# Placing the tiles of a hybrid decoder trunk at multiples of 128 bytes, with weight tiles stepped by 16 bytes from chunk to chunk

## The chip, the cores and the metric

The kernel runs on one core of one Trainium2 chip. The metric is the device time of one execution in microseconds. Three timed runs of the kernel before gave 645.31, 649.29 and 649.80 us, so the median is 649.29 us.

## The reference

The reference is a two-layer decoder trunk on one sequence of 256 tokens and 1024 features, all in float32. Layer 0 has an RMSNorm, one input projection shared by a softmax attention (8 heads of 64; with 256 tokens and blocks of 256 only the own causal block counts) and a gated linear attention (8 heads), one output projection and a residual add. Layer 1 has an RMSNorm, a projection to a gate branch and a recurrent branch (width-4 causal convolution, two block-diagonal gates, a linear recurrence over the tokens), an output projection and a residual add. After each of the two comes a gated feed-forward block, and it holds most of the arithmetic:

```
h = causal_dwconv(x @ w_up, conv_w, conv_b)      # 1024 -> 6144 columns, width 3
u, g = split(h, 2);  return (u * gelu(g)) @ w_down   # 3072 -> 1024
```

A final RMSNorm ends it. The weights are read once from device memory, some 107 MB in all.

## The kernel before

Activations lie transposed, features on the 128 partitions and the 256 tokens along the free dimension. All large weight matrices are cut on the host into 204 chunks of 128 partitions by 1024 float32 columns (4096 bytes of each partition) in the order in which they are used. A matrix product with close to float32 accuracy is made of three passes in the type fp32r: each weight chunk `w` is split into a high part `wh` (ScalarE, line 134) and a low part `wl = w - wh` (VectorE, line 135), the activations likewise into X[:, k, 0, :] and X[:, k, 1, :], and `passes` (lines 141 to 148) issues for each 128x128 block the products high-high, high-low and low-high. Each is one weight load of 128 columns (PEld in the profile) and one matmul with 256 moving columns (PE), so a chunk is 24 weight loads and 24 matmuls, and all 204 chunks are 4896 of the 5218 matmul records. In nearly all products the weight chunk is the stationary operand and the activations are the moving one; in `tok_gemm` (`pst` in the profile, 192 matmuls) it is the other way round.

`load_w` keeps a look-ahead of one chunk in program order; `issue_w` allocates the tiles: `w` from a ring of 4, `wh` and `wl` from rings of 6 each (a separate ring of 10 for the ten chunks from 104 on). Every transfer of a chunk goes through the queue of SP (line 127). The tile framework packs all tiles into the partition by their lifetimes. Within the rings it reuses addresses as they come free, and a tile that takes the place of another waits for the readers of that one. The order of instructions on each engine is set by the framework's own planner from its estimate of times, with a few orders forced by hand (`order`).

What the change touches is where tiles start. The framework places each tile at a multiple of 32 bytes. The tile `big` (line 80) is 2678 columns, 10,712 bytes, rounded to 10,720, which is 96 more than a multiple of 128. It starts at byte 98,432 of the partition (769 x 128), so what is packed directly behind it starts at byte 109,152, which is 852 x 128 + 96, and since chunks are 4096 bytes, all the `w`, `wh` and `wl` tiles in that region lie 96 bytes past a multiple of 128. A few chunks are placed ahead of `big`, in room that other tiles have left, and start at a multiple of 128. In the program as it is laid out:

| start past a multiple of 128 | chunks of 204 |
|---|---|
| `wh` 96, `wl` 96 | 174 |
| `wh` 96, `wl` 0 | 14 |
| `wh` 0, `wl` 96 | 6 |
| `wh` 0, `wl` 0 | 10 |

The ten are chunks 106, 124, 141, 147, 153, 159, 165, 171, 177 and 183; seven of them are in the up-projection of the second feed-forward block, one in every six chunks. The activations X, M and the `y2` of the feed-forward blocks all start at a multiple of 128 bytes, and every slice of them that a matmul reads does too.

Other tiles that the change touches are small: the 2-column tiles of the norms and the softmax (lines 189, 516, 521), the 8-column tiles of the recurrence constants (line 366) and one of 16 columns (line 576).

Of the kernel before, what the change touches and what calls it, by code (L numbers as in the profile page):

```python
# [8 lines left out]
F32 = mybir.dt.float32  # L9
F32R = mybir.dt.float32r  # L10
# [12 lines left out]
P = 128  # L23
S = 256
D = 1024
KT = 8
# [3 lines left out]
CW = 1024  # L30
# [18 lines left out]
NV = _o  # L49
# [13 lines left out]
def trunk(ctx: ExitStack, tc: tile.TileContext, xT, w, wgk, wgk2, vec, cst, mskf, out):  # L63
    nc = tc.nc

    cp = ctx.enter_context(tc.tile_pool(name="cp", bufs=1))
    wp = ctx.enter_context(tc.tile_pool(name="wp", bufs=4))
    xp = ctx.enter_context(tc.tile_pool(name="xp", bufs=1))
    tp = ctx.enter_context(tc.tile_pool(name="tp", bufs=2))
    pp = ctx.enter_context(tc.tile_pool(name="pp", bufs=1, space=bass.MemoryType.PSUM))  # L70

    def bank(name, tag="g"):
        return pp.tile([P, 512], F32, tag=tag, bufs=BANKS[tag], name=name)

    def order(first, then):
        tc.add_manual_dep(then.ins, first.ins.name,
                          mybir.DependencyInfo(mybir.DependencyClass.NoSync, mybir.DependencyReason.DATA),
                          reason="issue order")

    big = cp.tile([P, KT * S + P + NV + 8], F32, name="big")  # L80
    h = big[:, 0:KT * S].rearrange("p (k t) -> p k t", k=KT)
    idt = big[:, KT * S:KT * S + P]
    vt = big[:, KT * S + P:KT * S + P + NV]
# [22 lines left out]
    def act(name, *args, **kw):  # L106
        use(name)
        ins = nc.scalar.activation(*args, **kw)
        order(tbl["load"], ins)
        tbl["ops"].append(ins)  # L110
        return ins
# [6 lines left out]
    def load_w():  # L118
        while len(state["q"]) <= LOOK and state["i"] < NCH:
            state["q"].append(issue_w())  # L120
        return state["q"].pop(0)

    def issue_w():
        i = state["i"]
        state["i"] += 1
        wt = wp.tile([P, CW], F32, tag="w", name=f"w{i}")
        dma = nc.sync.dma_start(wt, w[i])
        if i == 0:
            first.append(dma)
        pre = "p" if L1_C0 <= i < L1_C0 + NPRE else ""  # L130
        nb = NPRE if pre else 6
        wh = wp.tile([P, CW], F32R, tag="wh" + pre, bufs=nb, name=f"wh{i}")
        wl = wp.tile([P, CW], F32R, tag="wl" + pre, bufs=nb, name=f"wl{i}")
        hi = nc.scalar.activation(wh, wt, AF.Copy)  # L134
        lo = nc.vector.tensor_sub(wl, wt, wh.bitcast(F32))  # L135
        for kind, o in (("h", hi), ("l", lo)):
            for before in state["hooks"].pop((kind, i), []):
                order(before, o)
        return wh, wl
# [24 lines left out]
    class Norm:  # L164
# [18 lines left out]
        def rstd(self, copy=True, hook=0):  # L183
            ps = bank("nps", "t")
            for t in range(2):
                for i, s_ in enumerate(self.acc):
                    nc.tensor.matmul(ps[:, t:t + 1], s_[:, t * P:(t + 1) * P], ones, start=i == 0,
                                     stop=i == len(self.acc) - 1)
            rt = tp.tile([P, 2], F32, tag="rtk", name="rtk")
            root = act(SQRT, rt, ps[:, 0:2], AF.Sqrt, bias=epst, scale=1.0 / D)  # L190
            inv = nc.vector.reciprocal(rt, rt)
            for t in range(2):
                nc.tensor.transpose(ps[:, S + t * P:S + (t + 1) * P], rt[:, t:t + 1].to_broadcast([P, P]), idt)
            self.tok = rt
            if not copy:
                return ps[:, S:2 * S]
            rs = tp.tile([P, S], F32, tag="rs", name="rs")
            cp_ = nc.scalar.activation(rs, ps[:, S:2 * S], AF.Copy)
            if hook:
                for key, o in zip((("h", hook), ("l", hook), ("h", hook + 1)), (root, inv, cp_)):  # L200
                    state["hooks"].setdefault(key, []).append(o)
            return rs
# [54 lines left out]
    for i in range(4):  # L257
        first.append(nc.sync.dma_start(h[:, 2 * i:2 * i + 2, :], xT[:, 2 * i:2 * i + 2, :]))
    state["q"].append(issue_w())
    first.append(nc.sync.dma_start(idt, cst[:, 0:P]))  # L260
    for a_, b_ in zip(first, first[1:]):
# [16 lines left out]
    with tc.tile_pool(name="l0", bufs=1) as lp, tc.tile_pool(name="l0r", bufs=4) as lr:  # L278
        def nt(name):
            return lr.tile([P, 512], F32, tag="n", bufs=14, name=name)  # L280

        state["q"].append(issue_w())
        state["q"].append(issue_w())
        gk2 = lp.tile([32, 256], F32, name="gk2")
# [78 lines left out]
        lam = vt[:, VOFF["lam"]:VOFF["lam"] + 8]  # L363

        def small(name):
            return cp.tile([P, 8], F32, name=name)

        e, d2, zz, z2, acc, cc = [small(f"s{i}") for i in range(6)]
        nc.scalar.activation(e, lam, AF.Abs)
        act(LNEXP, e, e, AF.Exp, scale=-1.0)  # L370
# [137 lines left out]
        def softmax(hd):  # L508
            m, r = hd // 2, slice(64 * (hd % 2), 64 * (hd % 2) + 64)
            q, k = rot["q", m // 2][:, m % 2, :], rot["k", m // 2][:, m % 2, :]  # L510
            ps = bank("pss", "s")
            nc.tensor.matmul(ps[:, 0:128], q[r, 0:P], k[r, 0:P], start=True, stop=False)
            nc.tensor.matmul(ps[:, 0:128], identb, caus, start=False, stop=True)
            nc.tensor.matmul(ps[:, 128:384], q[r, P:S], k[r, 0:S], start=True, stop=False)  # L514
            nc.tensor.matmul(ps[:, 256:384], identb, caus, start=False, stop=True)
            mx = lr.tile([P, 2], F32, tag="mx", name="mx")
            nc.vector.tensor_reduce(mx[:, 0:1], ps[:, 0:128], axis=mybir.AxisListType.X, op=ALU.max)
            nc.vector.tensor_reduce(mx[:, 1:2], ps[:, 128:384], axis=mybir.AxisListType.X, op=ALU.max)
            nc.vector.tensor_scalar(mx, mx, -0.125, None, op0=ALU.mult)
            pe = lr.tile([P, 384], F32, tag="pe", name="pe")  # L520
            sm = lr.tile([P, 2], F32, tag="sm", name="sm")
            act(LNEXP, pe[:, 0:128], ps[:, 0:128], AF.Exp, bias=mx[:, 0:1], scale=0.125, accum_out=sm[:, 0:1])
            act(LNEXP, pe[:, 128:384], ps[:, 128:384], AF.Exp, bias=mx[:, 1:2], scale=0.125, accum_out=sm[:, 1:2])
            nc.vector.reciprocal(sm, sm)
            nc.vector.tensor_scalar(pe[:, 0:128], pe[:, 0:128], sm[:, 0:1], None, op0=ALU.mult)
            nc.vector.tensor_scalar(pe[:, 128:384], pe[:, 128:384], sm[:, 1:2], None, op0=ALU.mult)
            pt = bank("ptr", "t")
            for b in range(3):
                nc.tensor.transpose(pt[:, b * P:(b + 1) * P], pe[:, b * P:(b + 1) * P], idt)
            p_ = lr.tile([P, 384], F32, tag="PT", name="PT", bufs=8)  # L530
            nc.scalar.activation(p_, pt[:, 0:384], AF.Copy)
            return p_
# [3 lines left out]
        for pr in range(4):  # L536
            for j in range(2):
                PT[2 * pr + j] = softmax(2 * pr + j)
            ps = bank("pso", "t")
            for j in range(2):  # L540
                hd = 2 * pr + j
                r = slice(64 * j, 64 * j + 64)
                cs = slice(64 * hd, 64 * hd + 64)
                nc.tensor.matmul(ps[r, 0:S], av[:, 0, cs], PT[hd][:, 0:S], start=True, stop=False)
                nc.tensor.matmul(ps[r, P:S], av[:, 1, cs], PT[hd][:, S:384], start=False, stop=True)
            split(M[:, pr, 0, :], M[:, pr, 1, :], ps[:, :S])
# [26 lines left out]
            gemm(ps[:, :S], load_w(), X)  # L573
            nc.vector.tensor_mul(bog[:, m, :], ps[:, :S], rs)
        act(SILU, bog, bog, AF.Silu)
        rh = lp.tile([P, 16], F32, name="rh")
        act(SQRT, rh, psn[:, 0:16], AF.Sqrt, bias=epst, scale=1.0 / 64)
        nc.vector.reciprocal(rh, rh)
        rb = lp.tile([P, 16, 64], F32, name="rb")
# [251 lines left out]
```

## Time and profile before

| | us |
|---|---|
| median of three runs | 649.29 |
| lowest and highest run | 645.31, 649.80 |
| the profiled execution | 646.74 |
| its span, first to last instruction | 645.0 |
| PE (matmul) busy | 630.7 (98%) |
| PEld (weight load) busy | 613.1 (95%) |
| DVE (VectorE) busy | 513.3 (80%) |
| ACT (ScalarE) busy | 406.0 (63%) |

The span is the time between the first and the last instruction of the program; the profiled execution's own time has 1.7 us more around it. Busy times of PE and PEld overlap each other, and a matmul's recorded duration overlaps the next one's, so the distance between successive starts says more of TensorE's pace than the durations do.

### The profile page before, as it was taken

How to read it: one execution, taken by the hardware profiler on the slowest of the kernel's cores; microseconds unless marked ns; L12 is line 12 of the kernel's file. 1: busy time of each engine (PE TensorE's matmuls, PEld its weight loads, DVE VectorE, ACT ScalarE, POOL GpSimd, SP SyncE). 2: the span in 40 equal slices, each digit the busy share in tenths (PEclk: the TensorE clock that was granted, in tenths of full speed). 3: DMA queues.
4: the chain of work that ended last, by engine and by line, in shares of the span. 5: the costliest groups of instructions: out<-in, count | busy, mean ns of one | idle time of the engine just before them, and what ended most of it. 6: DMA issues, size and time to landing. Idle time of an engine off the chain costs nothing.

```text
span 645.0 us, 12988 instructions
## 1 busy us (share of the span) xinstructions
PE 630.7 (98%) x5218; PEld 613.1 (95%) x5218; DVE 513.3 (80%) x902; ACT 406.0 (63%) x662; POOL 8.9 (1%) x36
## 2 busy tenths in 40 slices
PE   7999999999999999999999999989999999999995
PEld 4998888899999999999999999989999999999995
DVE  6699985467999999996577859996999999986532
ACT  7798454646776666675476578966666667674310
POOL 5000000000000000000000000000000000000000
PEclk8999999999999999999999999999999999999998
DMA  8823511534264485555277505544466545455201
GB/s 303 312 100 131 196 67 66 197 132 164 74 239 173 184 313 194 195 177 183 102 282 269 201 2 196 196 154 151 155 229 229 196 163 193 179 210 204 99 1 66
DMA packets 31516, 110.90 MB, mean 172 GB/s; under 512 B 3648, under 2 KB 4192, under 8 KB 31456
## 3 DMA queue, kind: packets, MB, share of 16 engines
q1 hardware_dynamic: 31456, 110.07, 47.5%
q8 instruction: 41, 0.67, 0.4%
q14 instruction: 19, 0.16, 0.1%
HBM read 109.01 MB, written 1.05 MB: 171 GB/s over the span
## 4 chain that ended last, share of the span: by engine, by line
PE 93%; DVE 2%; ACT 2%; issue 1%; DMA 1%; SPq 0%; DVEq 0%; ACTq 0%
PE psu L146 42%; PE psd L146 21%; PE psout L146 5%; PE psx L146 4%; PE psa L146 4%; PE pst L146 3%; PE psgb L146 3%; PE pl L465 2%; PE psog L146 2%; PE psgt L146 2%; PE psbq L146 1%; DVE wl L135 1%; PE psbk L146 1%; PE pss L514 1%; DMA big<-xT 1%
## 5 line engine op out<-in xcount | busy, mean ns | idle before, releaser
L134 ACT ACTIVATE wh<-w 128x1024 fp32r<-128x1024 f32 x204 | 212.5, 1056 | 112.8 <-PE psu L146 71.8
L135 DVE TENSOR_TENSOR wl<-w,wh 128x1024 fp32r<-128x1024 f32 x204 | 246.9, 1219 | 39.6 <-ACT wh L134 38.7
L146 PE MATMUL psu<-x,wh 128*128 128x256 f32 x1536 | 270.5, 280 | 0.0
L146 PEld LDWEIGHTS psu<-x,wh 128*128 128x128 f32 x1536 | 234.6, 189 | 0.0
L146 PE MATMUL psu<-x,wl 128*128 128x256 f32 x768 | 214.3, 280 | 0.0
L146 PEld LDWEIGHTS psu<-x,wl 128*128 128x128 f32 x768 | 144.7, 189 | 0.0
L146 PE MATMUL psd<-y,wh 128*128 128x256 f32 x768 | 134.6, 280 | 0.0
L146 PEld LDWEIGHTS psd<-y,wh 128*128 128x128 f32 x768 | 116.9, 188 | 0.0
L146 PE MATMUL psd<-y,wl 128*128 128x256 f32 x384 | 106.7, 279 | 0.0
L619 DVE SCALAR_TENSOR_TENSOR c<-v,big,c 128x255 f32<-128x255 f32 (+1 forms) x192 | 83.6, 475 | 0.0
L146 PEld LDWEIGHTS psd<-y,wl 128*128 128x128 f32 x384 | 72.1, 188 | 0.0
L617 ACT ACTIVATE c<-v,big 128x256 f32<-128x256 f32 x96 | 51.7, 589 | 0.6 <-DVE v L612 0.6
L172 ACT ACTIVATE sq<-big 128x256 f32<-128x256 f32 x40 | 15.4, 407 | 50.7 <-DVE big L211 50.6
L211 DVE TENSOR_TENSOR big<-big,psd 128x256 f32<-128x256 f32 x16 | 6.7, 420 | 35.3 <-PE psd L146 35.3
L612 DVE TENSOR_TENSOR v<-psu,rs 128x512 f32<-128x512 f32 x48 | 32.5, 681 | 0.0
L146 PE MATMUL psout<-r,wh 128*128 128x256 f32 x128 | 23.1, 282 | 2.0 <-DVE r L702 2.0
L146 PE MATMUL pst<-wh,x 128*128 128x256 f32 x128 | 24.2, 285 | 0.0
L146 PE MATMUL psout<-m,wh 128*128 128x256 f32 x128 | 23.7, 285 | 0.0
L146 PE MATMUL psx<-x,wh 128*128 128x256 f32 x128 | 23.0, 281 | 0.0
L146 PE MATMUL psgb<-x,wh 128*128 128x256 f32 x128 | 22.7, 280 | 0.0
L146 PE MATMUL psa<-x,wh 128*128 128x256 f32 x128 | 22.5, 280 | 0.0
L99 ACT ACT_TABLE_LOAD x17 | 21.8, 1283 | 1.0 <-PEq L823 0.7
(202 smaller groups left out, 850.5 us busy)
## 6 DMA issues: line engine op xcount, KB each, us to landing
w<-w SPq DMA_DIRECT2D x204, 512.0 KB, 4.3
big<-xT SPq DMA_DIRECT2D x4, 256.0 KB, 3.8
out<-o SPq DMA_DIRECT2D x4, 256.0 KB, 2.4
ct<-cst SPq DMA_DIRECT2D x1, 384.0 KB, 8.0
big<-vec SPq DMA_DIRECT2D x1, 224.0 KB, 7.9
mf<-mskf SPq DMA_DIRECT2D x1, 192.0 KB, 8.0
wg<-wgk SPq DMA_DIRECT2D x1, 64.0 KB, 2.0
big<-cst SPq DMA_DIRECT2D x1, 64.0 KB, 5.2
```

The costliest lines, as they stand in the source:

```text
L99: ld = nc.scalar.preload_act_table_set(name)
L134: hi = nc.scalar.activation(wh, wt, AF.Copy)
L135: lo = nc.vector.tensor_sub(wl, wt, wh.bitcast(F32))
L146: out.append(nc.tensor.matmul(ps, a, b, start=first and i + j == 0, stop=last and i == n - 1 and j == 2, skip_group_check=skip))
L172: ins = nc.scalar.activation(sq, t, AF.Square)
L211: nc.vector.tensor_add(h[:, m, :], h[:, m, :], ps)
L465: nc.tensor.matmul(pv[:, :, :, cs], Kb[li, I][:, ts_], qv[:, :, :, cs], start=True, stop=True)
L514: nc.tensor.matmul(ps[:, 128:384], q[r, P:S], k[r, 0:S], start=True, stop=False)
L612: nc.vector.tensor_mul(v, ps.rearrange("p (j t) -> p j t", j=2), rs[:, None, :].to_broadcast([P, 2, S]))
L617: nc.scalar.activation(c[:, j, :], v[:, j, :], AF.Identity, bias=V("fc_b", layer * 48 + ch), scale=wv(2))
L619: nc.vector.scalar_tensor_tensor(c[:, j, d:], v[:, j, 0:S - d], wv(2 - d), c[:, j, d:], op0=ALU.mult, op1=ALU.add)
```

## The change

Every tile whose size was not a multiple of 128 bytes is widened to one, so that all tiles start at a multiple of 128. `w`, `wh` and `wl` get 32 columns (128 bytes) more each, 4224 bytes in place of 4096. The `wh` and `wl` of chunk i are then the 1024 columns that start 4 * (i % 8) columns into their tiles: 0, 16, 32, 48, 64, 80, 96 or 112 bytes past a multiple of 128, the same for both. `w` stays at the start of its tile. The instructions and their sizes stay as they are.

```diff
-    big = cp.tile([P, KT * S + P + NV + 8], F32, name="big")
+    big = cp.tile([P, -(-(KT * S + P + NV + 8) // 32) * 32], F32, name="big")
...
-        wt = wp.tile([P, CW], F32, tag="w", name=f"w{i}")
+        wt = wp.tile([P, CW + 32], F32, tag="w", name=f"w{i}")[:, 0:CW]
...
-        wh = wp.tile([P, CW], F32R, tag="wh" + pre, bufs=nb, name=f"wh{i}")
-        wl = wp.tile([P, CW], F32R, tag="wl" + pre, bufs=nb, name=f"wl{i}")
+        oh, ol = 4 * (i % 8), 4 * (i % 8)
+        wh = wp.tile([P, CW + 32], F32R, tag="wh" + pre, bufs=nb, name=f"wh{i}")[:, oh:oh + CW]
+        wl = wp.tile([P, CW + 32], F32R, tag="wl" + pre, bufs=nb, name=f"wl{i}")[:, ol:ol + CW]
...
-            rt = tp.tile([P, 2], F32, tag="rtk", name="rtk")
+            rt = tp.tile([P, 32], F32, tag="rtk", name="rtk")[:, 0:2]
...
-            return cp.tile([P, 8], F32, name=name)
+            return cp.tile([P, 32], F32, name=name)[:, 0:8]
...
-            mx = lr.tile([P, 2], F32, tag="mx", name="mx")
+            mx = lr.tile([P, 32], F32, tag="mx", name="mx")[:, 0:2]
...
-            sm = lr.tile([P, 2], F32, tag="sm", name="sm")
+            sm = lr.tile([P, 32], F32, tag="sm", name="sm")[:, 0:2]
...
-        rh = lp.tile([P, 16], F32, name="rh")
+        rh = lp.tile([P, 32], F32, name="rh")[:, 0:16]
```

## Rows read from the trace of the kernel before

**Rows 1.** The page: busy times, the chain that ended last by engine.

```profile
PE 630.7 (98%) x5218; PEld 613.1 (95%) x5218; DVE 513.3 (80%) x902; ACT 406.0 (63%) x662; POOL 8.9 (1%) x36
...
PE 93%; DVE 2%; ACT 2%; issue 1%; DMA 1%; SPq 0%; DVEq 0%; ACTq 0%
```

**Rows 2.** The chain in order of time: start us, us, what.

```profile
161.79 121.57 PE psu L146 x1042
283.36 67.20 PE psd L146 x576
...
445.52 123.08 PE psu L146 x1047
568.60 67.52 PE psd L146 x576
```

**Rows 3.** Timeline, weight loads of chunk 145: start us, us, engine, what.

```profile
469.76 0.19 PEld L146 LDWEIGHTS psu<-x,wl 128*128 128x128 f32 x1
...
472.21 0.19 PEld L146 LDWEIGHTS psu<-x,wl 128*128 128x128 f32 x1
```

**Rows 4.** The same view, chunk 147.

```profile
475.37 0.19 PEld L146 LDWEIGHTS psu<-x,wl 128*128 128x128 f32 x1
...
477.88 0.19 PEld L146 LDWEIGHTS psu<-x,wl 128*128 128x128 f32 x1
```

**Rows 5.** Groups of weight loads, chunk 147 (475.28 to 477.95 us): busy us, mean ns.

```profile
L146 PEld LDWEIGHTS psu<-x,wh 128*128 128x128 f32 x16 | 2.5, 192 | 0.0
L146 PEld LDWEIGHTS psu<-x,wl 128*128 128x128 f32 x8 | 1.5, 192 | 0.0
```

**Rows 6.** The same view, chunk 145 (469.5 to 472.3 us).

```profile
L146 PEld LDWEIGHTS psu<-x,wl 128*128 128x128 f32 x9 | 1.7, 188 | 0.0
```

**Rows 7.** Busy time by stretch, chunks 141, 145, 147, 148: clock, DMA share, GB/s last.

```profile
458.31:461.07 2.76, 2.76 (x26) 2.76 (x24) 2.76 (x7) 1.24 (x3) 0.00 (x0) 1.00 0.01 3
469.57:472.37 2.80, 2.80 (x27) 2.80 (x26) 2.80 (x6) 2.05 (x3) 0.00 (x0) 1.00 0.71 263
475.25:478.00 2.75, 2.75 (x25) 2.75 (x24) 2.75 (x6) 2.05 (x3) 0.00 (x0) 1.00 0.61 223
478.12:480.86 2.74, 2.74 (x26) 2.74 (x24) 2.57 (x6) 1.68 (x3) 0.00 (x0) 1.00 1.02 396
```

**Rows 8.** Timeline, weight loads of chunk 141.

```profile
458.79 0.19 PEld L146 LDWEIGHTS psu<-x,wl 128*128 128x128 f32 x1
...
460.95 0.19 PEld L146 LDWEIGHTS psu<-x,wl 128*128 128x128 f32 x1
```

**Rows 9.** Timeline, weight loads of chunk 148.

```profile
478.24 0.19 PEld L146 LDWEIGHTS psu<-x,wl 128*128 128x128 f32 x1
...
480.73 0.19 PEld L146 LDWEIGHTS psu<-x,wl 128*128 128x128 f32 x1
```

**Rows 10.** Timeline, weight loads near 83 us, linear attention and tok_gemm.

```profile
82.61 0.53 PEld L465 LDWEIGHTS pl<-qb,kb 128*128 128x128 f32 x4
83.05 0.19 PEld L146 LDWEIGHTS pst<-wl,x 128*128 128x128 f32 x1
...
83.76 0.19 PEld L146 LDWEIGHTS pst<-wl,x 128*128 128x128 f32 x1
```

**Rows 11.** Groups of the splits, whole span: busy us, mean ns, idle before.

```profile
L135 DVE TENSOR_TENSOR wl<-w,wh 128x1024 fp32r<-128x1024 f32 x204 | 246.9, 1219 | 39.6 <-ACT wh L134 38.7
...
L134 ACT ACTIVATE wh<-w 128x1024 fp32r<-128x1024 f32 x204 | 212.5, 1056 | 112.8 <-PE psu L146 71.8 <-PE psd L146 17.4 <-issue 7.4
```

**Rows 12.** The splits by line, all 204: duration ns min/median/max, first and last start.

```profile
L135 DVE TENSOR_TENSOR wl<-w,wh x204: 1199/1220/1227, 10.4 to 619.6; 128x1024 fp32r<-128x1024 f32 x102
...
L134 ACT ACTIVATE wh<-w x204: 1041/1061/1099, 9.3 to 613.6; 128x1024 fp32r<-128x1024 f32 x102
```

**Rows 13.** Busy time by stretch, layer 0's mixer, its end, a feed-forward stretch.

```profile
50.00:75.00 25.00, 23.63 (x182) 21.98 (x181) 25.00 (x53) 16.32 (x34) 0.00 (x0) 1.00 0.49 173
75.00:100.00 25.00, 25.00 (x160) 19.83 (x159) 18.47 (x56) 12.47 (x35) 0.00 (x0) 1.00 0.28 102
100.00:125.00 25.00, 25.00 (x194) 21.47 (x194) 11.14 (x24) 13.17 (x29) 0.00 (x0) 1.00 0.35 127
...
200.00:250.00 50.00, 50.00 (x431) 50.00 (x430) 47.27 (x82) 33.39 (x56) 0.00 (x0) 1.00 0.59 222
```

**Rows 14.** Waits: engine, line, waited for, us, times, longest.

```profile
PE pst L146 <- DVE wl L135: 1.4, 1, 1.4
PE psbq L146 <- ACT wh L134: 0.9, 1, 0.9
...
SPq L127 <- DVE wl L135: 282.3, 84, 26.6
```

## The prediction

> **What bounds the kernel now.** I first read the page for the busiest engine and for the chain that ended last. TensorE's matmuls are busy 98% of the span, its weight loads 95%, and 93% of the chain is PE [rows 1]; the reader should see that no other engine's length matters unless it makes PE wait. Then the chain in order of time: the four long pieces are the feed-forward products, without a gap [rows 2]. Dividing gives TensorE's pace: 121.57 us / 1042 = 116.67 ns per matmul in the first up-projection, 67.20 / 576 = 116.67 ns in the first down-projection, but 123.08 / 1047 = 117.55 ns and 67.52 / 576 = 117.22 ns in the second layer [rows 2]. The instructions are the same; what differs is where some weight chunks lie. So I read the timeline of weight loads chunk by chunk. Chunk 145, both split halves 96 bytes past a multiple of 128: from its first `wl` load shown to the last, 21 loads on, 472.21 - 469.76 = 2.45 us, 116.7 ns each [rows 3]. Chunk 147, both halves on a multiple of 128: 477.88 - 475.37 = 2.51 us, 119.5 ns [rows 4]. The recorded load grows with it, 188 ns on average in the one and 192 ns in the other [rows 6, 5].
>
> Is it the place and not something that happens beside it? The clock is fully granted in all these stretches. The DMA engines were 71% busy beside the fast chunk 145, 61% beside the slow 147, and 1% beside chunk 141 [rows 7], which also lies on a multiple of 128 and takes (460.95 - 458.79) / 18 = 120.0 ns [rows 8]. Chunk 148, with `wh` at 96 and `wl` at 0, has 2.49 us / 21 = 118.6 ns [rows 9]. So the start of the weights matters by 2.8 ns per load: 0 is dear, 96 is cheap. Whether what counts is the start of the weights themselves or their distance from the moving activations (all on multiples of 128), the trace does not settle: near 83 us, where the chunk is the moving operand and the activations at 0 are the weights, the pace is (83.76 - 83.05) / 6 = 118.3 ns [rows 10], dear again either way.
>
> **The change, part by part.** *Weights at eight offsets.* 4896 matmuls take a chunk. Two of the eight offsets are known: 96 costs 116.67 ns, 0 costs 119.5 ns, an excess of 2.83 ns. Before, the excess is the ten chunks at 0 (10 x 24 x 2.83 = 0.68 us) and the twenty mixed ones (20 x 24 x (118.6 - 116.67) = 0.93 us), 1.6 us in all; read from the chain instead: (117.55 - 116.67) x 1047 + (117.22 - 116.67) x 576 = 1.2 us for the second feed-forward block, which holds most of them. After, 612 matmuls have each offset. Offset 0: 612 x 2.83 = 1.7 us. Offset 96: nothing. The six others are unseen and the trace bounds them only from afar. From above, the dearest chunk seen, 120.0 ns [rows 8], an excess of 3.3 ns. From below, the loads of `pl`, 128 columns each beside a shorter matmul: (83.05 - 82.61) / 4 = 110 ns [rows 10], 6.7 ns less than at 96. I take the middle of the seen: 16 and 112, next to the dear one, half as dear (2 x 612 x 1.4 = 1.7 us), the other four like 96. The reason to choose near 96: 174 of 204 chunks run at a pace so even (116.67 ns in two stages with different activations) that it looks like a plain rate, with 0 as the disturbed case. Sum: 1.7 + 1.7 - 1.6 = +1.8 us. The ends, six offsets at 3.3 ns and six at -6.7 ns: 12.1 + 1.7 - 1.6 = +12.2 us and -24.6 + 1.7 - 1.6 = -24.5 us.
>
> [...]
>
> *Splits at other offsets.* ACT and DVE now write `wh` and `wl` at steps of 16 bytes and read them so. The splits at 0 and at 96 are all inside 1199 to 1227 ns on DVE and 1041 to 1099 ns on ACT [rows 12], so the start does not show. I cost it at nothing; the cover is that DVE waits 38.7 us for `wh` and ACT 89 us for PE to free a buffer before a split [rows 11]. Were each 5% longer, 61 ns x 204 = 12 us on DVE would lie beside PE's work, and only the waits of PE for a split, 1.4 + 0.9 us [rows 14], would grow.
>
> *`w` at a multiple of 128 in place of 96.* Its transfers are issued where a split has freed a buffer (282.3 us of SP's waits [rows 14]), well ahead of need; nothing on the path.
>
> *Room.* `w`, `wh` and `wl` take 3% more, the small tiles 64 to 120 bytes more each, and everything is packed anew. Ring depths stay, so the feed-forward blocks (431 matmuls in 50 us, PE full [rows 13]) keep their slack. In layer 0's mixer PE is not full: 182, 160 and 194 matmuls in 25 us where a full one has 215 [rows 13]. There a new overlap of addresses can make a wait, or remove one. Bound: 1 to 3 us either way, from the single waits of 1.4 us seen there [rows 14]; I take 0 as I know no sign.
>
> *Float32 operands of the attention.* The blocks of the linear attention move from 96 to 0. Some 250 loads by at most 3.3 ns is under 1 us, off the full stretches; I add 0.5.
>
> Sum +2.3 us. Against the profiled execution, 646.7 us (span 645.0 and 1.7 around it), that is 649; against the median of the runs, 2.6 us higher, 651.6. I say 650.
>
> **The rivals.** *Most offsets are dear.* If 96 is the lucky one, the other six cost what 0 does: 7 x 612 x 2.83 - 1.6 = +10.5 us, 660 from the median (657 from the profiled execution). The place is every weight load of the two feed-forward blocks, and it decides from the point where the mean excess over the eight passes (6.5 + 1.6) us / 4896 = 1.65 ns: four or five of them like 0. For: of the seen starts, only one is cheap, and all others (0 with 0, 0 with 96, weights at 0 under a moving chunk) lie at 118.3 to 120.0 ns. Against: the exact rate at 96. Chance 0.33.
>
> *Some offsets are cheaper than 96.* With three of the six at 110 ns the kernel gains 3 x 612 x 6.7 - 1.7 + 1.6 = 12 us, 637; two at that price reach -8 us. For: a load can be done in 110 ns [rows 10]. Against: nothing with 256 moving columns runs below 116.67 ns. Chance 0.14.
>
> *The place counts for nothing* and the slow chunks are slow because of the room ahead of `big`, not because of the 128 bytes. Then all chunks return to 116.67 ns: -1.6 us, 648. [...] Against: dear weights lie in two distant places there. Within no change; 0.1 of its chance.
>
> *The waits of layer 0's mixer* move by 3 us or less; it shifts every case and decides none.
>
> **How the numbers follow.** 1% is 6.5 us, about what a measurement can tell from no change. My forecast and the rival of no effect fall within it: 0.53 together (0.43 and 0.10). Slower by over 1%: 0.33. Faster by over 1%: 0.14. The time is 650. The range reaches up to all six dear with 2 us of new waits, 662, and down to two offsets at 110 ns from the median, 640; outside are three or more cheap offsets, and offsets dearer than any seen. The likeliest case alone spans 645 to 655, the runs' own spread included.
>
> **What would show it.** Pace by chunk in the feed-forward blocks should go round in eights: about 119.5 ns where i % 8 = 0 and 116.7 where i % 8 = 6, with recorded loads of 192 and 188 ns. The six others are the question: mean pace of the long psu pieces below 118 ns, I am right; 119 ns, the first rival; below 115.5, the second. All eight at 116.7: the place counted for nothing. Longer splits than 1227 ns on DVE, or new waits of PE for `wl`, would show the covered costs surfacing. I am wrong above all if the dear offsets are the rule, or if the stretch from 50 to 125 us grows by more than 3 us.

## The result and the profile after

The changed kernel took 655.19 us in the median of four runs (653.96 to 657.03), the kernel before 647.42 us in the four runs beside it: a ratio of 1.0118, 95% interval 1.0084 to 1.0153. It is slower by a little over 1%. The profiled execution took 653.96 us with a span of 652.2 us, 7.2 us more than before.

The page, busy times and the chain that ended last by engine, answering to [rows 1]:

```profile
PE 637.1 (98%) x5218; PEld 619.4 (95%) x5218; DVE 515.1 (79%) x902; ACT 408.7 (63%) x662; POOL 8.9 (1%) x36
...
PE 89%; DMA 4%; DVE 2%; ACT 2%; issue 1%; SPq 0%; DVEq 0%; ACTq 0%
```

PE's instructions are as many as before and it is busy 6.4 us longer; 4% of the chain is now a transfer, where it was 1%. The chain's long pieces in order of time (start us, us, what), answering to [rows 2]:

```profile
161.00 123.48 PE psu L147 x1042
284.48 44.94 PE psd L147 x380
...
451.13 123.80 PE psu L147 x1047
574.93 68.19 PE psd L147 x576
```

The four paces are 118.50, 118.26, 118.24 and 118.39 ns per matmul, against 116.67, 116.67, 117.55 and 117.22. The two layers now agree, and every piece is slower than its counterpart. Measured from first matmul to first matmul (layer 1's mixer from its first weight load, 0.1 us earlier), the stages changed by these amounts:

| stage | before us | after us | difference |
|---|---|---|---|
| layer 0, mixer | 137.73 | 136.83 | -0.9 |
| first up-projection | 135.07 | 137.15 | +2.1 |
| first down-projection | 67.09 | 68.05 | +1.0 |
| layer 1, mixer | 82.12 | 85.53 | +3.4 |
| second feed-forward block | 203.42 | 204.94 | +1.5 |
| tail | 9.13 | 9.35 | +0.2 |

**The weights.** Weight loads in the timeline of the changed kernel (start us, us, engine, what), first and last of 22 in a row. Chunk 54, offset 96, answering to [rows 3]:

```profile
210.50 0.19 PEld L147 LDWEIGHTS psu<-x,wl 128*128 128x128 f32 x1
...
212.99 0.19 PEld L147 LDWEIGHTS psu<-x,wl 128*128 128x128 f32 x1
```

Chunk 44 and then chunk 164, both with offset 64:

```profile
182.09 0.19 PEld L147 LDWEIGHTS psu<-x,wl 128*128 128x128 f32 x1
...
184.59 0.19 PEld L147 LDWEIGHTS psu<-x,wl 128*128 128x128 f32 x1
...
529.62 0.19 PEld L147 LDWEIGHTS psu<-x,wl 128*128 128x128 f32 x1
...
532.01 0.19 PEld L147 LDWEIGHTS psu<-x,wl 128*128 128x128 f32 x1
```

Over 21 loads that is 118.6 ns for the offset 96, which cost 116.7 before, and 119.0 and 113.8 ns for one and the same offset, 64. So the start past a multiple of 128 doesn't set the pace. Taking every chunk's pace from its starts and averaging by offset over the feed-forward chunks gives, within 0.1 ns, 118.5, 118.6, 119.9, 118.3, 117.0, 117.9, 118.3 and 118.6 ns for 0, 16, ... 112. Yet it is no noise: within a block the pace repeats every 24 chunks, which is where eight offsets and six buffers come round together. Chunks 39, 63 and 87 each have 120.0 ns, 40 and 64 118.6, 42 and 66 121.0. What counts is more of a chunk's address than its remainder by 128. Before, nearly all chunks had the same place by a larger measure too, because six tiles of 4096 bytes all leave the same remainder by 1024; tiles of 4224 bytes don't.

**Layer 1's start.** The windows (us, then busy us and count of PE, PEld, DVE, ACT, POOL, granted clock, DMA share, GB/s), kernel before, then after:

```profile
340.00:365.00 25.00, 25.00 (x216) 25.00 (x215) 19.67 (x28) 14.91 (x21) 0.00 (x0) 1.00 0.77 274
```

```profile
340.00:365.00 25.00, 23.24 (x196) 22.84 (x195) 17.89 (x21) 16.66 (x20) 0.00 (x0) 1.00 0.86 294
```

Twenty matmuls fewer are 2.4 us at 118 ns. The chain there, kernel before, is PE without a gap:

```profile
350.56 4.71 PE psx L146 x40
...
359.73 0.22 PE nps L193 x2
```

In the changed kernel it runs through transfers of weights:

```profile
339.31 5.21 DMA w<-w
...
348.25 0.11 DVE ssq L180
348.37 5.51 DMA w<-w
...
356.21 0.11 DVE big L212
356.32 5.03 DMA w<-w
...
361.43 1.07 ACT wh L135
...
362.53 0.18 DVE wl L136
...
363.67 0.17 DVE rtk L192
...
363.88 0.43 PE nps L194 x2
```

Read it upwards: the norm's product `nps` waits for DVE's `rtk`, which stands on DVE behind a split `wl`, which waits for ACT's `wh` and that for the transfer of `w`, and the transfers stand in the chain right behind DVE's `ssq` and `big`, whose work ahead of them gave up the address (that it is the address is read from the order of the rows, not tried). The product comes at 363.88 in place of 359.73. Before, PE waited once for `rtk`, 0.6 us; now it is 1.5 us in two waits, and the wait of `psx` for the activations is new. PE's and SP's waits (us in total, times, longest), answering to [rows 14]:

```profile
PE nps L194 <- DVE rtk L192: 1.5, 2, 1.0
...
PE psx L147 <- ACT x L206: 0.8, 1, 0.8
```

```profile
SPq L127 <- DVE wl L136: 327.2, 119, 27.0
```

**The splits**, answering to [rows 12] (durations ns min/median/max, first and last start, forms), stayed as they were, 1226 ns in the median against 1220 on DVE and 1062 against 1061 on ACT:

```profile
L136 DVE TENSOR_TENSOR wl<-w,wh x204: 1204/1226/1244, 10.3 to 626.4; 128x1024 fp32r<-128x1024 f32 x102
```

```profile
L135 ACT ACTIVATE wh<-w x204: 1038/1062/1074, 9.2 to 622.3; 128x1024 fp32r<-128x1024 f32 x102
```

### The profile page after: what moved, and what is told of

The parts are those of the page before. It is cut to its first block, busy times and chain, and to the rows that moved or that the text cites. A ratio compares the mean times of both kernels' runs of the same rounds, so it can differ in the third digit from the quotient of the medians.

```text
span 652.2 us, 13063 instructions
## 1 busy us (share of the span) xinstructions
PE 637.1 (98%) x5218; PEld 619.4 (95%) x5218; DVE 515.1 (79%) x902; ACT 408.7 (63%) x662; POOL 8.9 (1%) x36
## 4 chain that ended last, share of the span: by engine, by line
PE 89%; DMA 4%; DVE 2%; ACT 2%; issue 1%; SPq 0%; DVEq 0%; ACTq 0%
PE psu L147 42%; PE psd L147 17%; PE psout L147 5%; PE pst L147 4%; PE psa L147 4%; PE psgb L147 3%; DMA w<-w 3%; PE psx L147 2%; PE pl L466 2%; PE psog L147 2%; PE psgt L147 2%; DVE wl L136 1%; ACT wh L135 1%; PE psbq L147 1%; PE psbk L147 1%
## 5 line engine op out<-in xcount | busy, mean ns | idle before, releaser
L136 DVE TENSOR_TENSOR wl<-w,wh 128x1024 fp32r<-128x1024 f32 x204 | 248.6, 1225 | 62.8 <-ACT wh L135 61.6
L147 PE MATMUL psu<-x,wh 128*128 128x256 f32 x1536 | 273.4, 281 | 0.0
L147 PE MATMUL psd<-y,wh 128*128 128x256 f32 x768 | 136.2, 281 | 0.0
```

The source lines that it names most:

```text
L147: out.append(nc.tensor.matmul(ps, a, b, start=first and i + j == 0, stop=last and i == n - 1 and j == 2, skip_group_check=skip))
```

## The experiments

The first three take the change apart. All three, and the survey after them, ran beside the same eight runs of the kernel before (median 649.36 us).

**No steps.** The changed kernel with every chunk at offset 0.

```diff
-        oh, ol = 4 * (i % 8), 4 * (i % 8)
+        oh, ol = 0, 0
```

> The changed kernel with every wh and wl at the start of its tile: no 16-byte steps, all else as changed (tiles of 4224 bytes, all starts at multiples of 128, the same addresses for the same chunks). Theory A, the start past a multiple of 128 sets the pace: all 4896 loads at the dear 0, by the trace of before (119.6 ns) +12 us against before, about 660 us, by the trace of after (118.5 ns) +7 us, 654. Theory B, the steps themselves cost (successive chunks at other offsets): back to about the kernel before, 647 to 650. Theory C, what counts is where hi, lo and the moving activations lie to each other modulo more than 128 bytes, and the 4224-byte tiles scatter that: pace near 118.4 ns in the mean, 653 to 655, whatever the steps.

657.16 us (655.92 to 658.62), ratio 1.0132, interval 1.0096 to 1.0168. The chain:

```profile
163.29 123.86 PE psu L147 x1042
...
455.51 124.20 PE psu L147 x1047
```

118.87 and 118.62 ns, not the 119.5 ns of offset 0 before, and some 0.4 ns above the changed kernel; the ratio agrees with the changed kernel's within the intervals, and the time is 2 us above what theory C gave. Taking the steps away changes almost nothing: they were neither the cost nor a gain worth naming. In this program as it is laid out a start at a multiple of 128 is 0 or 128 modulo 256, counted from the activations, and that shows: chunks with both halves at 0 run at 119.8 ns, with both at 128 at 118.5.

**Alignment alone.** All tiles at multiples of 128, but `w`, `wh` and `wl` at 4096 bytes and without steps. Against the changed kernel:

```diff
-        wt = wp.tile([P, CW + 32], F32, tag="w", name=f"w{i}")[:, 0:CW]
+        wt = wp.tile([P, CW], F32, tag="w", name=f"w{i}")[:, 0:CW]
...
-        oh, ol = 4 * (i % 8), 4 * (i % 8)
-        wh = wp.tile([P, CW + 32], F32R, tag="wh" + pre, bufs=nb, name=f"wh{i}")[:, oh:oh + CW]
-        wl = wp.tile([P, CW + 32], F32R, tag="wl" + pre, bufs=nb, name=f"wl{i}")[:, ol:ol + CW]
+        oh, ol = 0, 0
+        wh = wp.tile([P, CW], F32R, tag="wh" + pre, bufs=nb, name=f"wh{i}")[:, oh:oh + CW]
+        wl = wp.tile([P, CW], F32R, tag="wl" + pre, bufs=nb, name=f"wl{i}")[:, ol:ol + CW]
```

> The alignment alone: big and the small tiles widened as in the change, but w, wh and wl of 4096 bytes and without steps, so that hi and lo of nearly all chunks have one and the same place modulo 1024, on a multiple of 128. Theory A by the trace of after (0 costs 118.5 ns): about 654 us; theory C (an equal pair at distance 0 from the activations, modulo 128, is what the ten slow chunks of before had): 119.5 to 119.7 ns in the feed-forward blocks, 658 to 661 us. Theory B: 647.

659.0 us (658.19 to 662.53), ratio 1.017, interval 1.0127 to 1.0214.

```profile
162.05 125.03 PE psu L147 x1042
...
452.85 125.62 PE psu L147 x1047
```

120.0 ns in both: an exact pace again, as 116.67 was, but a dearer one, with every pair of the feed-forward blocks at one place, distance 0 from the activations modulo 256. It is the place of the ten dear chunks of before, of which the eight in the feed-forward blocks ran at 119.2 to 119.7 ns; the 174 even ones of before are at 224.

**Wider tiles alone.** The kernel before with 32 columns more in `w`, `wh` and `wl`, nothing aligned, no steps.

```diff
...
-        wh = wp.tile([P, CW], F32R, tag="wh" + pre, bufs=nb, name=f"wh{i}")
+        wh = wp.tile([P, CW + 32], F32R, tag="wh" + pre, bufs=nb, name=f"wh{i}")[:, 0:CW]
...
```

> The kernel before with nothing but w, wh and wl widened to 4224 bytes: big is not widened, no steps, so chunks still start 96 bytes past a multiple of 128 but hi and lo lie at scattered places modulo 1024. Theory A by the trace of before (96 is cheap, 116.67 ns): 645 to 648 us, as before. Theory C: the even 116.67 ns is lost, mean pace near 118 ns, 651 to 655 us.

654.35 us (653.61 to 655.82), ratio 1.0092, interval 1.0061 to 1.0124.

```profile
162.86 122.60 PE psu L146 x1042
...
450.76 124.03 PE psu L146 x1047
```

117.66 and 118.46 ns. Every weight still starts 96 or 0 past a multiple of 128, as before, and the pace has gone all the same. Together: alignment alone +1.7%, width alone +0.9%, both +1.3%, both with steps +1.2%. They don't add up, which fits that none is a cost of its own and each only moves the weights away from the place they had.

**Survey of places.** One kernel in which the activations start at multiples of 1024 and the two halves of three successive chunks at a time lie at a chosen distance past a multiple of 1024. Rings of five slots of 5120 bytes hold the halves.

```diff
-            wh = wp.tile([P, CW], F32R, tag="wh" + pre, bufs=nb, name=f"wh{i}")
-            wl = wp.tile([P, CW], F32R, tag="wl" + pre, bufs=nb, name=f"wl{i}")
+            s_ = (i if i < L1_C0 else i - NPRE) % 5 * 1280
+            oh, ol = PLACE.get(i, REST)
+            wh = ring_h[:, s_ + oh:s_ + oh + CW]
+            wl = ring_l[:, s_ + ol:s_ + ol + CW]
...
```

> A survey of places: wh and wl in two fixed rings of five slots, activations at multiples of 1024 bytes, and the place of wh and wl modulo 1024 set by hand, the same for three chunks in a row. First up-projection: both at the same place, 0, 32, ... 480. First down-projection: both at 16, 80, ... 464. Second up-projection: wh at 960, wl at 0, 64, ... 960. Second down-projection: eight pairs. Theory A: each start modulo 128 has one pace, 480 and 96 alike. Theory C: the pace changes with the place modulo 512 or 1024 and with the pair; 480 with 480 has 116.67 ns as the chunks of before (608 with activations at 128), 0 with 0 has 119.6, and 960 with 320 has 113.3 ns, as the fastest chunks of the changed kernel (wh 64, wl 448, activations at 128). A total between 640 and 665 us.

One run, 655.84 us. Weight loads of chunk 38 (both halves at 64) and chunk 66 (both at 352), first and last of 31:

```profile
171.31 0.19 PEld L159 LDWEIGHTS psu<-x,wlring 128*128 128x128 f32 x1
...
174.71 0.19 PEld L159 LDWEIGHTS psu<-x,wlring 128*128 128x128 f32 x1
...
250.12 0.19 PEld L159 LDWEIGHTS psu<-x,wlring 128*128 128x128 f32 x1
...
253.72 0.19 PEld L159 LDWEIGHTS psu<-x,wlring 128*128 128x128 f32 x1
```

113.3 and 120.0 ns, with the same instructions and the clock fully granted. All distances with both halves equal, pace in ns from the starts of each chunk (of three chunks, the mean; at 0 and 32 in the first row PE's break for the norm falls among them):

| distance | 0 | 32 | 64 | 96 | 128 | 160 | 192 | 224 |
|---|---|---|---|---|---|---|---|---|
| pace | 119.65 | 118.2 | 113.4 | 120.0 | 118.7 | 119.9 | 117.8 | 117.75 |
| 256 further | 120.1 | 118.3 | 113.4 | 120.0 | 118.7 | 119.9 | 117.8 | 117.75 |

The second row repeats the first: the pace goes by the distance from the activations modulo 256. With 16, 80, 144 and 208 (down-projection) it was 118.3, 118.5, 116.67 and 116.67; 256 further 118.3, 118.6, 120.0 and 116.67, so 144 had two prices. With `wh` held at 960, `wl` at 0, 64, 128, 192 gave 117.8, 113.3, 115.55, 117.8, and so again up to 960, but for the first three chunks, which lie about the break: the pair counts, not each half by itself. The place 480 is the distance of the kernel before; it gave 117.75 where the kernel before has 116.67. That was a miss.

**Two ways to the distance 64.** If distance were all, the kernel before should reach 113.3 ns either by weights 96 bytes further on or by activations 160 further on. First the weights (the room ahead of them grows):

```diff
-    big = cp.tile([P, KT * S + P + NV + 8], F32, name="big")
+    big = cp.tile([P, KT * S + P + NV + 8 + 24], F32, name="big")
```

> The kernel before with big widened by 24 columns (96 bytes) and nothing else: the 174 chunks behind it now start 64 bytes past a multiple of 256, counted from the activations (576 in place of 480 bytes modulo 1024). Theory C (the distance of weights and activations modulo 256 sets the pace; the survey had 113.33 ns at 64 and 117.75 at 224 with an equal pair): 174 x 24 matmuls at 113.3 in place of 116.7 ns, 14 us less than before, a ratio of 0.976 to 0.982. Theory A (the start past a multiple of 128 alone; the chunks of the changed kernel at 64 had 117.0 ns in the mean): within 2 us of before.

650.1 us in the median of twelve (644.07 to 653.3), ratio 1.0027, interval 1.0001 to 1.0054. No gain.

```profile
160.00 122.73 PE psu L146 x1042
```

117.78 ns. Then the activations, each in a tile 256 bytes larger:

```diff
-        return xp.tile([P, KT, 2, S], F32R, tag="x", name="x")
+        return xp.tile([P, KT * 2 * S + 64], F32R, tag="x", name="x")[:, 40:40 + KT * 2 * S].rearrange("p (k j t) -> p k j t", k=KT, j=2)
```

(and so for M and `y2`.)

> The other way round: the weights keep their starts (171 chunks 96 past a multiple of 128), and the activations X, M and y2 lie 160 bytes into tiles of 256 bytes more, so that the weights are again 64 bytes past a multiple of 256 counted from the activations. Theory C, the distance: 113.3 ns in the feed-forward blocks, about 14 us less than before. Theory D, the weights' own address: 116.7 ns and a time within 2 us of before.

639.18 us (637.97 to 643.15), ratio 0.9866, interval 0.984 to 0.9892.

```profile
440.39 122.10 PE psu L146 x1047
562.49 65.88 PE psd L146 x576
```

The second block's means are 116.62 and 114.37 ns, but by chunk it is a mixture. In the first block chunks 32, 34 and 36, ahead of PE's break for the norm, run at 117.6 to 117.9 ns and all from 37 to 103 at 113.33. Weight loads of chunks 40 and 41, 42 from first to last, 113.3 ns:

```profile
169.08 0.19 PEld L146 LDWEIGHTS psu<-x,wl 128*128 128x128 f32 x1
...
173.84 0.19 PEld L146 LDWEIGHTS psu<-x,wl 128*128 128x128 f32 x1
```

In the second block, chunks 137 to 140 run at 117.8; from 147 on, in the up-projection, two of every six have 113.3 to 113.5, and the others, three with one or both halves elsewhere and the one behind them, 114.1 to 120.1. The odd ones with both halves at distance 96 have 120.0, as in the survey, where weights and activations both lay elsewhere: the distance tells more than the weights' own address. With the same distance, one kernel has 117.79 throughout its feed-forward blocks and the other mostly 113.33. As a theory, distance alone had fallen. The kernel with the weights further on shows both paces itself: in the mixer of layer 0 its chunks 5 to 11 run at 113.3 ns.

**Everything at 64**, every weight tile at a multiple of 256 and the activations 192 past one, so that no chunk differs.

```diff
-        wh = wp.tile([P, CW], F32R, tag="wh" + pre, bufs=nb, name=f"wh{i}")
+        wh = wp.tile([P, CW], F32R, tag="wh" + pre, bufs=nb, name=f"wh{i}", align_bytes=256)
...
-        return xp.tile([P, KT, 2, S], F32R, tag="x", name="x")
+        return xp.tile([P, KT * 2 * S + 64], F32R, tag="x", name="x", align_bytes=256)[:, 48:48 + KT * 2 * S].rearrange("p (k j t) -> p k j t", k=KT, j=2)
...
```

> All weight tiles at multiples of 256 bytes, 4096 bytes long, and the activations 192 bytes past a multiple of 256, so that every chunk, those ahead of big too, is 64 bytes past a multiple of 256 from the activations. Theory C: 113.3 ns for nearly all of the 4704 matmuls with the chunk as weights, 17 to 18 us less than before, a ratio of 0.971 to 0.977, 2 to 4 us below the kernel with big widened. Theory A: the dear 0, 119.5 ns, 12 us more than before.

646.04 us in the median of twelve, ratio 0.9966, interval 0.9935 to 0.9998, far from the 0.971 to 0.977 expected. The twelve fall in two groups, six from 641.99 to 643.72 us and six from 648.37 to 650.68; the profiled one is of the second. Its weight loads ahead of PE's break for the norm near 157 us, then in chunks 50 and 51:

```profile
155.32 0.19 PEld L146 LDWEIGHTS psu<-x,wl 128*128 128x128 f32 x1
...
156.34 0.19 PEld L146 LDWEIGHTS psu<-x,wl 128*128 128x128 f32 x1
...
198.10 0.19 PEld L146 LDWEIGHTS psu<-x,wl 128*128 128x128 f32 x1
...
201.99 0.19 PEld L146 LDWEIGHTS psu<-x,wl 128*128 128x128 f32 x1
```

Ahead of the break 1.02 us over 9 loads, 113.3 ns; after it 3.89 us over 33, 117.9 ns, and so without exception to the end of the block, and again after the same break in layer 1. Modulo 512 the chunks of an up-projection all have one place. So one place has two steady paces, and the stream can change from one to the other at a break; within a block it didn't leave its pace by itself.

**Steps with both halves alike.** The change's eight offsets, in the survey's rings, so that both halves and the activations keep one distance.

```diff
-            oh, ol = PLACE.get(i, REST)
+            oh, ol = 4 * (i % 8), 4 * (i % 8)
```

> The steps alone, without the scatter of the 4224-byte tiles: wh and wl in two rings of five slots at multiples of 1024 bytes, both 16 * (i % 8) bytes on, activations at multiples of 1024. Five slots cost some 10 us of waits in the mixers (the survey had 73 us outside the steady pace, before 64), so only the pace of the feed-forward blocks is compared. If the distance modulo 256 sets the pace whatever the tile size: by the survey 0 has 119.7, 16 118.4, 32 118.2, 64 113.3 or 117.8, 80 118.6 and 96 120.0 ns, so a mean of 117.9 to 118.8. If the steps cost nothing by themselves and only the scatter does: about 117 ns.

One run, 657.77 us. By offset, 0 to 112: 119.8, 118.4, 118.3, 117.75, 113.5, 118.8, 117.2 and 119.9 ns (the median of 18 chunks each). The chain has

```profile
165.34 124.18 PE psu L153 x1052
```

118.04 ns. So the steps by themselves cost what they do in the changed kernel (118.3), and one cheap offset in eight doesn't pay for the other seven. Offset 96 had 117.2 ns here and 120.0 in the survey, entered from other neighbours: another place with two prices.

**A kick.** If the stream keeps its pace until something jolts it, a single odd chunk after the break should bring it back. Everything at 64, and `wl` of chunks 36, 84, 136 and 184 another 32 bytes on.

```diff
+        if i in KICK:
+            wl = wp.tile([P, CW + 64], F32R, tag="wlk", bufs=1, name=f"wl{i}", align_bytes=256)[:, 8:8 + CW]
...
```

> The kernel with every chunk at distance 64 (modulo 256), with the wl of chunks 36, 84, 136 and 184 lying 32 bytes further on. At distance 64 three kernels showed two steady paces, 113.33 and 117.79 ns, and changed over at a break in the stream or at a chunk whose halves lie 64 and 96 off. Theory E, the pace depends on the state in which the stream enters: after chunk 36 and after 136 the feed-forward blocks run at 113.3 ns (the kernel without these four had 117.8 from chunk 35 on), 15 us less than that kernel, ratio to before 0.97 to 0.98. Theory F, the state is set by the absolute addresses of this layout: 117.8 ns as without them, ratio 0.995 to 1.0.

641.1 us (639.1 to 642.54), ratio 0.9894, interval 0.9867 to 0.9921. Chunks 37 to 83 stayed at 117.79 ns: chunk 36 is worked through beside 32 and 34, largely ahead of the break, and so comes too early. Chunk 84 turned the stream to 113.33: 27 loads ahead of it and 27 behind it, 117.8 and 113.3 ns:

```profile
288.27 0.19 PEld L150 LDWEIGHTS psd<-y,wl 128*128 128x128 f32 x1
...
291.45 0.19 PEld L150 LDWEIGHTS psd<-y,wl 128*128 128x128 f32 x1
...
301.24 0.19 PEld L150 LDWEIGHTS psd<-y,wl 128*128 128x128 f32 x1
...
304.30 0.19 PEld L150 LDWEIGHTS psd<-y,wl 128*128 128x128 f32 x1
```

In layer 1 the stream turned at the end of chunk 136, whose last four loads come behind the break; the break itself is a rival there.

```profile
447.85 118.74 PE psu L150 x1047
```

113.41 ns.

**The kick after the break**, both halves of chunks 40, 84 and 140 at distance 48.

```diff
+        if i in KICK:
+            wh = wp.tile([P, CW + 64], F32R, tag="whk", bufs=1, name=f"wh{i}", align_bytes=256)[:, 60:60 + CW]
+            wl = wp.tile([P, CW + 64], F32R, tag="wlk", bufs=1, name=f"wl{i}", align_bytes=256)[:, 60:60 + CW]
...
```

> Every chunk at distance 64 (modulo 256), but chunks 40, 84 and 140 with both halves at 48. With the steps at equal pairs the step from 48 to 64 ended in the fast pace in 15 of the 18 chunks. Theory E, the state in which the stream enters decides: the kernel with four kicks stayed at 117.8 ns from chunk 35 to 84 because its kick, chunk 36, runs interleaved with chunks 32 and 34, before the break at chunk 35; a kick at chunk 40 comes after it, so chunks 41 to 79 run at 113.3 to 113.6 ns, some 4 us less than that kernel, ratio to before 0.979 to 0.987. Theory G, the first block cannot hold the fast pace (its place or its neighbours): 117.8 ns again in chunks 41 to 79 and a ratio near 0.989.

634.91 us (631.82 to 644.23), ratio 0.9795, interval 0.9761 to 0.9829, faster than both kernels.

```profile
163.47 114.82 PE psu L151 x1012
...
440.20 116.19 PE psu L151 x1024
```

113.46 and 113.47 ns. So the first block can hold the cheap pace, which one theory denied. But the trace doesn't show that the kicks brought it. Chunk 40 starts at 169.11 us, and the loads of chunks 38 and 39 ahead of it are already on the cheap pace, 45 from first to last:

```profile
163.89 0.19 PEld L151 LDWEIGHTS psu<-x,wl 128*128 128x128 f32 x1
...
168.99 0.19 PEld L151 LDWEIGHTS psu<-x,wl 128*128 128x128 f32 x1
```

That is 113.3 ns. The stream fell to 117.8 at one break near 157.5 us and came back a few loads behind the next, at 163 us. Chunks 81 and 83 ahead of the second kick and 138 and 139 ahead of the third run at 113.3 ns too. In this execution the three odd chunks only cost their own 117.7 to 118.0 ns; the pace went on behind them as it was. They have tiles of their own, so the packing changed with them, and why this kernel comes out of the breaks on the cheap pace and the one without kicks didn't is open. One of its six runs took 644.23 us, the others 631.82 to 636.39; that run has no profile, so its pace is not shown.

## Why the prediction was right or wrong

- **What bounds the kernel: right.** PE's pace sets the end, and what moved in the feed-forward blocks moved by pace. PE is busy throughout 165 to 300 and 455 to 610 us, so no length of a split or transfer shows there.
- **The step that failed: "Two of the eight offsets are known: 96 costs 116.67 ns, 0 costs 119.5 ns."** They were known for one place of the tiles, 224 and 0 modulo 256 from the activations, not for a remainder by 128. With wider tiles alone, weights still at 96 and 0, the pace is 117.66 to 118.46 ns; in the changed kernel chunk 54 at offset 96 costs 118.6 in place of 116.7 [rows 3]. In its place the runs show: the pace goes by the distance of both halves from the activations modulo 256 (in the survey 113.4 ns at 64 and 320, 120.0 at 96 and 352), and differs by what came before (with everything at 64, 113.3 ns ahead of a break and 117.9 behind it). The trace of before held a sign of it. It showed an exact pace in 174 chunks that all shared one place; I read its evenness as "a plain rate, with 0 as the disturbed case", but with alignment alone the weights, all at another single place, run as evenly at 120.0. Evenness told of sameness, not of an undisturbed rate.
- **The term.** The offsets were put at +1.8 us. The mean pace over all 4896 matmuls that take a chunk rose from 117.08 to 118.31 ns, which is 6.0 us. In the feed-forward pieces of the chain the paces give 1.91 + 0.92 + 0.72 + 0.67 = 4.2 us of it. The upper bound, 12.2 us, held; the choice of the middle was too low. No run isolates the 0.5 us put in for the attention's float32 operands.
- **"Most offsets are dear"** came near by size: it decides at a mean excess of 1.65 ns, and the excess over 116.67 was 1.64. Its reason, that 96 is lucky and the others cost what 0 does, fell with the rest: 96 lost its luck and 0 became cheaper (119.5 to 118.5). The psu pieces, 118.50 and 118.24 ns, lie between the forecast's mark of 118 and the rival's of 119.
- **"Some offsets are cheaper than 96"** holds for one place, 64 (113.3 to 113.8 ns in chunks 60, 148, 164 and 172 of the changed kernel), and not always there (119.0 ns in chunk 44); the others outweigh it.
- **"The place counts for nothing"** is refuted by alignment alone, 120.0 against 116.67 ns. Nor is it the weights' place alone: moving only the activations by 160 bytes took the pace from 116.67 to mostly 113.33 ns.
- **Splits at nothing: right.** 1226 against 1220 ns and 1062 against 1061, and DVE still has idle time ahead of its splits, 62.8 us, 61.6 of it for `wh`. **`w` at nothing** held for its start at a multiple of 128: with alignment alone the chain at layer 1's start is `psx` without a transfer of `w`. Whether it held for its width is not shown, as the next point has it.
- **Room: no sign was known, and the place was wrong.** Layer 0's mixer, where I put 1 to 3 us either way, gained 0.9. The wait came at the start of layer 1, which the prediction did not look at: 20 matmuls fewer in 25 us, 2.4 us, because transfers now wait for DVE there; over the span SP waits for DVE's `ssq` 37.3 us in 15 waits, 26.7 in 9 before. Which part of the change brings it is not shown: transfers lie in the chain there with wider tiles alone (5.73, 4.38 and 4.78 us) and without steps (5.64 and 5.85), not with alignment alone, but again with tiles of 4096 bytes and everything at 64 (4.74 and 5.48). Layer 1's mixer takes 84.47 us with wider tiles alone, 86.87 without steps, 83.52 with alignment alone, 82.12 before.
- **The numbers.** 650 was forecast, 655.19 measured, inside the range of 640 to 662. The case "slower by over 1%", at 0.33, is what came; the likeliest one, no change, did not. The sum had +2.3 us where 7.8 us came, and that the time lies in the range is owed to the range's width and not to the price by offset.

What stays open: why distance modulo 256 matters (no run separates the load's reads from the moving operand's), why one place has two steady paces, and which jolts switch them. That the kernel with weights 96 further on stayed at 117.79 ns because it entered on the dear pace fits the kernels with everything at 64, and its chunks 129 to 131, ahead of the second block, do run at 113.3 ns. But not every odd chunk brings the cheap pace back: in that kernel chunk 141 has both halves at distance 0 and 142 has `wl` there, and 143 to 146 stayed at 117.8 ns, and so did all at 64 through the block. And its chunk 132, with `wh` at 0, took the stream from 113.3 to 117.9 ns.

## What to carry to other kernels

Where TensorE runs without a gap, write out its start-to-start time per load and matmul and ask whether it is the least that this shape shows anywhere; here 113.33 to 120.0 ns, 6%, hung on where two operands lie to each other and on the pace that the stream came in on. A remainder found in one layout is not a law: vary both operands' places before trusting it, and when a pace is even, ask whether all chunks share a place, as they did here at 116.67 ns before and at 120.0 with alignment alone. A change of tile sizes repacks everything, so look for new waits at each stage's start, not only where there was slack; here layer 1's mixer grew by 3.4 us.

## What was not expected of the hardware

- Weight load and matmul of 128 by 128 and 256 columns in fp32r ran for whole chunks at paces that come back exactly in other kernels, 113.33, 116.67, 117.79 and 120.0 ns among them (120.0 with alignment alone, in the survey and in three chunks of the changed kernel), all at a granted clock of 1.00 from 165 to 300 and from 455 to 610 us.
- One place had two steady paces, 113.33 or 117.79 ns, each kept over dozens of chunks; where it changed, a break or an odd chunk lay there. From 165 to 280 us a recorded load is 188 ns on average with the activations 160 further on, mostly on the first pace, and 190 (`wh`) and 188 (`wl`) with everything at 64, on the second. In the changed kernel, where 24 loads in a row come at 113.2 to 113.5 ns each, it is 110.1 ns from the start of a load to that of its matmul, and 115.0 where they come at 117.7 to 117.85.
- A kernel with every chunk at one place took 0.9966 of the time before; with three chunks of 204 moved by 16 bytes, into tiles of their own, it took 0.9795. The difference is clear, the moved chunks as its cause are not shown.
